# Two transformer blocks on one core: a raised priority for the attention strips' vector and scalar work, and half of each stacked key tile copied by DMA

## The chip, the cores and the metric

The kernel runs on one core of a Trainium2 chip. Its engines work side by side, each through its own instructions in order: TensorE (PE, with its weight loads as PEld), VectorE (DVE), ScalarE (ACT), GpSimd (POOL) and SyncE (SP, which here only issues DMAs). The metric is the device time of one execution in microseconds (us); lower is better.

## What is computed

A first block and then a second one run over a sequence of 512 positions with a model width of 1024; the sums are in float32. The first block has softmax attention with 8 heads of 64 columns beside a gated unit, the second has 8 heads of banded "chunk attention" (ca) and 8 heads of latent attention (mla). Each block ends in a convolutional feed-forward network. Cut to what matters here:

```python
def forgetting_attention(q, k, v, log_f):            # block 1, 8 heads of 64
    logits = einsum('bqhd,bkhd->bhqk', qi, k) * scale + ci[..., None] - c_k
    logits = where(causal, logits, -inf)
    p = softmax(logits); return einsum('bhqk,bkhd->bqhd', p, v)

def chunk_attention(q, k, v, rel_bias):              # block 2, 8 heads of 64; q, k are normed
    s = einsum('bqhd,bkhd->bhqk', qch, kb) * scale + bias[None]
    p = softmax(where(valid, s, NEG_INF)); return einsum(..., p, vb)

def second_block(...):
    q = rmsnorm_2(x w_q ...); k = ...; o_mla = mla_attention(q, k, v)
    cq, ck = rmsnorm_2(ca[0]), rmsnorm_2(ca[1]); o_ca = chunk_attention(cq, ck, cv, rel_bias)
    x = x + g_a * concat(o_mla, o_ca) @ w_out;  ...conv feed-forward...
```

## The kernel before

**Matrix products.** Every large product is made of three products of fp32r parts: a float32 matrix is split into a high part (`whi`, `xnh`) and the rest (`wlo`, `xnl`), and high·high, high·low and low·high are summed in PSUM (L369 is the one line that issues matmuls). ACT casts the high part of a weight piece (L347), DVE or POOL subtracts for the low part (L348). SP loads the raw pieces into three `wraw` buffers (L338).

**Attention strips.** A strip is one head and 128 query rows, `qi` 0 to 3, with 128 to 512 keys. In the order of time a strip is: the score matmuls (`strip_scores`, `s<-kh,qs` and `s<-kl,qs`), a DVE pass that adds the bias and takes the row minimum (L590, `s<-s,bs`, in an order's rows ISA, in the profile CUSTOM_DVE_ANT_0), the exponential on ACT (L594, `p<-s,st`), transposes on PE (L603, `s<-ident,p`), a copy to SBUF on ACT or DVE, whichever the scheduler gives it to (L605, `pt<-s`), and the product with the values (`o<-vc,pt`). `attention` walks over all strips. In turn t it issues the scores of strip t, then half of its `fill`, the transposes of strip t-1, the other half of `fill`, and the values of strip t-2. `fill` is a list of other matrix products (in block 2: `cq1`, `ck1`, `mla0`, `cv1`, `mla1`, parts of the output projection), and `rate(t)` says how many ns of it a turn takes. `bg` is a list of background work on DVE, ACT and POOL, above all norms; `bg` runs 60 places behind in priority. A norm ends in a power on POOL (`rsqrt`, L523), between a scale on DVE and the products on DVE that use it (`ca<-ca,ssc` L1423, `mqk<-mqk,nw` L1514).

**Stacked heads.** In block 1 and for the ca heads, `stack` builds for each head `qs` (high part of q in one half of the partitions, low part in the other), `kh` (the high part of k in both halves) and `kl` (the low part of k in both halves). Each half is 64 partitions by 512 floats, 128 KB. Head h is prepared `ahead` strips before its first strip: 2 in block 1, 4 in block 2.

**What sets the order.** PE runs in the order of the program. On the other engines a scheduler sets the order when the program is built: it takes the ready instruction of the best priority by its own estimates of time. On the chip each engine then runs that order strictly, so an instruction that waits holds up all behind it.

## Time and profile before

| | |
|---|---|
| median of 3 runs | 1244.67 us (1243.74 to 1245.11) |
| the profiled execution's own time | 1242.75 us |
| its span, first to last instruction | 1240.9 us |
| mean granted TensorE clock | 0.989 |
| TensorE matmul busy | 97% of the span |
| VectorE, ScalarE, GpSimd busy | 64%, 43%, 16% |

All times in rows are microseconds from the start of the span. Idle time of an engine counts only where PE, the engine that is nearly always busy, waits for it. A row's "granted clock" (PEclk) of 1.00 is 2.4 GHz and of 0.50 is 1.2 GHz.

### The profile page before, as it was taken

Reading aid. Unit: us, or ns where it says so; the run is one execution under the profiler, and the core shown is the slowest. Engines: PE = TensorE matmul, PEld = TensorE weight load, DVE = VectorE, ACT = ScalarE, POOL = GpSimd, SP = SyncE. Lnnn points to the kernel's source line nnn. Section 1 sums busy time; section 2 is a strip of 40 time slices with the busy share of each in tenths; the row PEclk is TensorE's granted clock in tenths of the full one; section 3 lists DMA queues with packets and bytes.
Section 4 is the critical chain, followed back from the end, with each engine's and each line's share of the span. In section 5 each row is a group of like instructions: output and inputs, shape, how many; then the busy total and the mean of one; then the engine's idle time right before and its main releaser. Section 6 shows DMA issues by size and latency. Waiting matters only on the chain.

```text
span 1240.9 us, 17330 instructions
## 1 busy us (share of the span) xinstructions
PE 1206.9 (97%) x6730; PEld 1049.5 (85%) x6730; DVE 792.5 (64%) x1415; ACT 539.2 (43%) x963; POOL 194.2 (16%) x208
## 2 busy tenths in 40 slices
PE   9999999999999999999998998899999999999998
PEld 6887878988888888888998897789988888888887
DVE  6555877688888886433666779766676566553221
ACT  6444544444444443223435555664554444442110
POOL 1457400300000000000344452501200000000000
PEclk9999999999999999999999999999999999999999
DMA  7321212156666656433122111110132222233330
GB/s 242 99 86 48 73 68 69 52 190 200 189 202 195 193 185 193 129 94 114 56 103 64 56 69 61 51 35 18 69 119 87 101 102 92 96 94 103 117 110 17
DMA packets 40033, 131.57 MB, mean 106 GB/s; under 512 B 4608, under 2 KB 5504, under 8 KB 39952
## 3 DMA queue, kind: packets, MB, share of 16 engines
q1 hardware_dynamic: 31536, 102.64, 25.2%
q10 hardware_dynamic: 8208, 27.27, 7.1%
q8 instruction: 52, 0.85, 0.3%
q0 software_dynamic: 208, 0.57, 0.2%
q14 instruction: 29, 0.24, 0.1%
HBM read 128.37 MB, written 2.10 MB: 105 GB/s over the span
## 4 chain that ended last, share of the span: by engine, by line
PE 85%; DVE 7%; POOL 4%; ACT 2%; issue 2%; DMA 1%; SPq 0%; POOLq 0%; ACTq 0%; DVEq 0%
PE mm L369 74%; PE s L369 4%; PE o L369 3%; PE s L603 2%; DVE wlo L348 1%; DVE nt L550 1%; DMA x<-in_xT_dram 1%; DVE ca L1423 1%; DVE s L590 0%; POOL ss L523 0%; POOL nw L523 0%; PE s L695 0%; DVE kl L669 0%; DMA cs<-in_c_dram 0%; PE mm L1635 0%
## 5 line engine op out<-in xcount | busy, mean ns | idle before, releaser
L348 DVE TENSOR_TENSOR wlo<-wraw,whi 128x1024 fp32r<-128x1024 f32 (+4 forms) x182 | 210.4, 1158 | 182.0 <-ACT whi L347 181.2
L347 ACT CAST whi<-wraw 128x1024 fp32r<-128x1024 f32 (+4 forms) x194 | 192.2, 994 | 281.3 <-PE mm L369 261.8
L369 PE MATMUL mm<-xnh,whi 128*128 128x512 f32 (+1 forms) x832 | 312.4, 375 | 1.1 <-DVE nt L550 0.6
L369 PE MATMUL mm<-xnl,whi 128*128 128x512 f32 (+1 forms) x832 | 311.0, 374 | 0.0
L369 PE MATMUL mm<-xnh,wlo 128*128 128x512 f32 (+1 forms) x832 | 310.7, 373 | 0.0
L369 PEld LDWEIGHTS mm<-xnh,whi 128*128 128x128 f32 x832 | 157.0, 189 | 28.7 <-PE mm L369 0.8
L369 PEld LDWEIGHTS mm<-xnh,wlo 128*128 128x128 f32 x832 | 157.1, 189 | 27.7
L369 PEld LDWEIGHTS mm<-xnl,whi 128*128 128x128 f32 x832 | 157.2, 189 | 27.1
L369 PE MATMUL mm<-gh,whi 128*128 128x512 f32 (+1 forms) x384 | 141.6, 369 | 1.1 <-DVE x L937 0.6
L369 PE MATMUL mm<-gl,whi 128*128 128x512 f32 (+1 forms) x384 | 141.3, 368 | 0.0
L369 PE MATMUL mm<-gh,wlo 128*128 128x512 f32 (+1 forms) x384 | 141.3, 368 | 0.0
L729 DVE SCALAR_TENSOR_TENSOR cv<-mm,cols,cv 128x510 f32<-128x510 f32 (+1 forms) x176 | 130.4, 746 | 2.6 <-ACT cv L727 0.6
L369 PE MATMUL mm<-whi,xnh 128*128 128x256 f32 (+3 forms) x304 | 97.7, 321 | 0.2 <-ACT xnh L812 0.2
L369 PE MATMUL mm<-wlo,xnh 128*128 128x256 f32 (+3 forms) x304 | 94.3, 310 | 0.2 <-DVE wlo L348 0.2
L369 PE MATMUL mm<-whi,xnl 128*128 128x256 f32 (+3 forms) x304 | 94.2, 310 | 0.1
L369 PEld LDWEIGHTS mm<-gh,whi 128*128 128x128 f32 x384 | 72.4, 188 | 13.6 <-DVE x L937 0.8
L369 PEld LDWEIGHTS mm<-gl,whi 128*128 128x128 f32 x384 | 72.4, 188 | 12.1
L369 PEld LDWEIGHTS mm<-gh,wlo 128*128 128x128 f32 x384 | 72.4, 188 | 12.0
L594 ACT ACTIVATE p<-s,st 128x128 f32<-128x128 f32 (+1 forms) x96 | 50.7, 528 | 69.7 <-DVE st L590 66.7
L998 DVE CUSTOM_DVE_ANT_0 wada<-wada,cs,cols 128x1024 f32<-128x1024 f32 x48 | 61.5, 1282 | 26.9 <-DMA wada<-in_w_ada_dram 26.7
L369 PE MATMUL mm<-mix,whi 128*128 128x256 f32 (+1 forms) x288 | 74.4, 346 | 2.7 <-ACT vm L1563 1.2
L727 ACT ACTIVATE cv<-mm,cols 128x512 f32<-128x512 f32 x88 | 67.6, 772 | 0.2 <-PE mm L369 0.2
(293 smaller groups left out, 1839.1 us busy)
## 6 DMA issues: line engine op xcount, KB each, us to landing
wraw<-in_w_up_dram SPq DMA_DIRECT2D x88, 512.0 KB, 3.4
wada<-in_w_ada_dram ACTq DMA_DIRECT2D x48, 512.0 KB, 3.6
wraw<-in_w_down_dram SPq DMA_DIRECT2D x32, 512.0 KB, 3.5
wraw<-in_w_out_dram SPq DMA_DIRECT2D x16, 512.0 KB, 3.4
wraw<-in_w_down_dram SPq DMA_DIRECT2D x16, 384.0 KB, 3.1
wraw<-in_w_qk_dram SPq DMA_DIRECT2D x8, 512.0 KB, 3.7
wraw<-in_w_v_dram SPq DMA_DIRECT2D x8, 256.0 KB, 4.9
x<-in_xT_dram SPq DMA_DIRECT2D x8, 256.0 KB, 6.4
```

What stands on the lines that cost most here:

```text
L347: nc.scalar.copy(hi[:, :n], raw[:, :n])
L348: (nc.gpsimd if pool else nc.vector).tensor_tensor(out=lo[:, :n], in0=raw[:, :n], in1=hi[:, :n].bitcast(F32), op=ALU.subtract)
L369: self.nc.tensor.matmul(out, lhsT, rhs, start=start, stop=stop, **kw)
L550: self.applied = nc.vector.scalar_tensor_tensor(out=t, in0=x[k][:, cs], scalar=gain(k), in1=r, op0=ALU.mult, op1=ALU.mult).ins
L594: nc.scalar.activation(out=p[:, :nk], in_=s[:, :nk], func=AF.Exp, bias=st[:, len(parts) - 1:len(parts)], scale=-1.0, accum_out=hd["sums"](qi))
L603: self.nc.tensor.transpose(s[:, c], p[:, c], self.ident)
L727: nc.scalar.activation(out=t, in_=ps, func=AF.Identity, scale=w[2], bias=self.col(cb, n))
L729: nc.vector.scalar_tensor_tensor(out=t[:, d:], in0=ps[:, :512 - d], scalar=w[2 - d], in1=t[:, d:], op0=ALU.mult, op1=ALU.add)
L998: nc.vector.tensor_tensor_reduce(out=w, in0=w, in1=self.cs, scale=1.0, scalar=self.col("b_ada_2", n), op0=ALU.mult, op1=ALU.add, accum_out ...
L1423: nc.vector.tensor_tensor(out=v3, in0=v3, op=ALU.mult, in1=ss[:, j, z, t].unsqueeze(2).to_broadcast([P, 4, 64]))
```

## The change

Four things change. (1) The DVE pass, the exponential, the copy `pt` and the two instructions that end a pair of heads (`reciprocal` and `att`) are recorded with a priority 150 places ahead. (2) In `stack`, the second half of `kh` and of `kl` is no longer computed by ACT and DVE but copied from the first half by a DMA on SP's queue. (3) In block 2, three rounds of 1200 ns of `fill` and 800 ns of `bg` are issued ahead of the attention, and (4) the fill between the first head's preparation and its first strip is 1500 ns instead of 3000 ns.

```diff
+FIRST = 150
 BEHIND = 60
...
-        for j, (cs, b) in enumerate(parts):
-            nc.vector.tensor_tensor_reduce(
...
-        p = self.pp.tile([P, 512], F32, tag="p", name="p")
-        nc.scalar.activation(out=p[:, :nk], in_=s[:, :nk], func=AF.Exp, bias=st[:, len(parts) - 1:len(parts)],
-                             scale=-1.0, accum_out=hd["sums"](qi))
+        with self.tc.high_priority(offset=FIRST):
+            for j, (cs, b) in enumerate(parts):
+                nc.vector.tensor_tensor_reduce(
...
+            p = self.pp.tile([P, 512], F32, tag="p", name="p")
+            nc.scalar.activation(out=p[:, :nk], in_=s[:, :nk], func=AF.Exp,
...
-        self.nc.any.tensor_copy(out=pt[:, :nk], in_=s[:, :nk])
+        with self.tc.high_priority(offset=FIRST):
+            self.nc.any.tensor_copy(out=pt[:, :nk], in_=s[:, :nk])
...
-        for o in (a, b):
-            nc.scalar.copy(kh[o], k[a])
-            nc.vector.tensor_tensor(out=kl[o], in0=k[a], in1=kh[a].bitcast(F32), op=ALU.subtract)
+        nc.scalar.copy(kh[a], k[a])
+        nc.vector.tensor_tensor(out=kl[a], in0=k[a], in1=kh[a].bitcast(F32), op=ALU.subtract)
+        for t in (kh, kl):
+            nc.sync.dma_start(out=t[b].bitcast(F32), in_=t[a].bitcast(F32))
...
-        nc.vector.reciprocal(sums[:, c8], sums[:, c8])
         att = self.att.tile([P, 512], F32, tag="att", name="att")
...
+        with self.tc.high_priority(offset=FIRST):
+            nc.vector.reciprocal(sums[:, c8], sums[:, c8])
+            nc.vector.tensor_tensor(out=att[:, c512].rearrange("p (g d) -> p g d", d=64),
...
+        for _ in range(3):
+            fill.run(1200)
+            bg.run(800)
         self.attention(
             heads, fill,
-            lambda t: 3000 if t < 0 else 2000 if t < 16 else 1600 if t < 34 else 500,
+            lambda t: 1500 if t < 0 else 2000 if t < 16 else 1600 if t < 34 else 500,
```

Three places in the orders of the engines show what moves: the norm of `ck1` on DVE and POOL, the preparation of a later pair of heads on DVE, and SP's queue. On PE the same instructions are issued; in block 2 there are 30 matmuls of 256 columns between the transposes of the first pair of heads (`mm<-ident,ca`) and the first score before, and 12 in the change, where 36 others have moved ahead of these transposes.

DVE in block 2, at the norm of `ck1`, before (`s<-s,bs` is a strip's bias pass, 128 to 512 keys wide; `ssc` is the norm's statistic):

```order
L590 ISA s,st<-s,bs 128x128
L590 ISA st 128x1
L348 TENSOR_TENSOR wlo<-wraw,whi 128x256
L1606 TENSOR_SCALAR bs<-bs 128x512
L1435 COPY ca<-mm 128x256 x2
L590 ISA s,st<-s,bs 128x256
...
L1412 TENSOR_REDUCE ssc<-sqc 128x4 x2
L1418 TENSOR_SCALAR ssc<-ssc 128x16
L1423 TENSOR_TENSOR ca<-ca,ssc 128x256 x3
L687 TENSOR_TENSOR att<-o,sums 128x512
L590 ISA s,st<-s,bs 128x384
```

The same place in the change:

```order
L592 ISA s,st<-s,bs 128x128
L592 ISA st 128x1
L1424 TENSOR_SCALAR ssc<-ssc 128x16
L1492 COPY mqk<-mm 128x384
L1429 TENSOR_TENSOR ca<-ca,ssc 128x256
L1612 TENSOR_SCALAR bs<-bs 128x512
L1429 TENSOR_TENSOR ca<-ca,ssc 128x256 x3
L592 ISA s,st<-s,bs 128x256
...
L1492 COPY mqk<-mm 128x384 x2
...
L693 TENSOR_TENSOR att<-o,sums 128x512
L592 ISA s,st<-s,bs 128x384
```

The norm stands one strip earlier, and the strip of 256 keys now stands behind its products instead of ahead of them.

POOL at the norm of `ck1`, before (`sqc` are its squares, `ssc<-ssc,nhalf` is its power, `wlo` the low part of a weight piece):

```order
L1411 TENSOR_TENSOR sqc<-ca 128x256 x2
L1607 MEMSET bs 64x64
L1411 TENSOR_TENSOR sqc<-ca 128x256 x2
L348 TENSOR_TENSOR wlo<-wraw,whi 128x1024
L523 TENSOR_TENSOR ssc<-ssc,nhalf 128x16
L348 TENSOR_TENSOR wlo<-wraw,whi 128x1024
```

The same place in the change:

```order
L1417 TENSOR_TENSOR sqc<-ca 128x256 x4
L524 TENSOR_TENSOR ssc<-ssc,nhalf 128x16
L349 TENSOR_TENSOR wlo<-wraw,whi 128x1024
L1613 MEMSET bs 64x64
L349 TENSOR_TENSOR wlo<-wraw,whi 128x1024
```

The power stands ahead of the weight split instead of behind it.

DVE a little later in block 2, where the third pair of ca heads (`qf`, `qs`, `kl`) is prepared, before:

```order
L1599 COPY qf<-mm 128x512
L348 TENSOR_TENSOR wlo<-wraw,whi 128x1024
L1606 TENSOR_SCALAR bs<-bs 128x512
L666 TENSOR_TENSOR qs<-qf,qs 64x512
L669 TENSOR_TENSOR kl<-kf,kh 64x512 x2
L590 ISA s,st<-s,bs 128x128
L590 ISA st 128x1
L590 ISA s,st<-s,bs 128x256
```

The same place in the change (`x` are products of the final norm of block 1):

```order
L1605 COPY qf<-mm 128x512
L592 ISA s,st<-s,bs 128x128
L592 ISA st 128x1
L349 TENSOR_TENSOR wlo<-wraw,whi 128x1024
L609 COPY pt<-s 128x512
L1612 TENSOR_SCALAR bs<-bs 128x512
L670 TENSOR_TENSOR qs<-qf,qs 64x512
L672 TENSOR_TENSOR kl<-kf,kh 64x512
L918 SCALAR_TENSOR_TENSOR x_83<-x_83,cols,mm 128x256
L918 SCALAR_TENSOR_TENSOR x_84<-x_84,cols,mm 128x256
L918 SCALAR_TENSOR_TENSOR x_85<-x_85,cols,mm 128x256
L592 ISA s,st<-s,bs 128x256
```

The strip of 128 keys has moved ahead of the weight split and of the head's preparation; the strip of 256 keys stands behind them and behind three products.

SP at the last two ca heads in the change, where before eight loads of `w_out` follow each other without a DMA between them (`kh<-kh` and `kl<-kl` are the new copies):

```order
L339 DMA wraw<-in_w_out_dram 128x1024 x4
L674 DMA kh<-kh 64x512
L674 DMA kl<-kl 64x512
L674 DMA kh<-kh 64x512
L339 DMA wraw<-in_w_out_dram 128x1024
L674 DMA kl<-kl 64x512
L339 DMA wraw<-in_w_out_dram 128x1024
```

The last head's `kl` copy stands behind a weight load that itself waits for a free `wraw` buffer.

## Rows read from the trace of the kernel before

**Rows 1.** The page: busy time, share of the span, instructions of an engine.

```profile
PE 1206.9 (97%) x6730; PEld 1049.5 (85%) x6730; DVE 792.5 (64%) x1415; ACT 539.2 (43%) x963; POOL 194.2 (16%) x208
```

**Rows 2.** Stretch, us, busy of PE, PEld, DVE, ACT, POOL; PEclk, DMA share, GB/s.

```profile
62.00:212.00 150.00, 142.10 (x804) 121.06 (x804) 101.67 (x252) 72.96 (x159) 55.52 (x53) 0.97 0.21 67
...
656.00:670.00 14.00, 10.60 (x76) 9.99 (x75) 11.30 (x14) 7.41 (x13) 5.19 (x3) 0.88 0.06 20
670.00:730.00 60.00, 54.90 (x423) 53.64 (x422) 43.19 (x100) 30.62 (x75) 29.94 (x34) 0.95 0.20 65
...
730.00:786.00 56.00, 48.55 (x329) 43.69 (x329) 49.02 (x112) 33.08 (x80) 20.81 (x22) 0.97 0.22 76
```

**Rows 3.** Waits of PE, 656 to 786: total us, times, longest.

```profile
PE s L603 <- ACT p L594: 8.6, 5, 2.9
PE mm L1596 <- DVE ca L1423: 3.4, 2, 2.2
```

**Rows 4.** Timeline of PE around the first score of block 2: start, length.

```profile
661.73 1.66 PE L1596 MATMUL mm<-ident,ca 128*128 128x128 f32 x6 [2.17 <-DVE ca L1423]
...
665.64 0.28 PE L369 MATMUL mm<-whi,xnh 128*128 128x256 f32 x1
...
667.57 0.28 PE L369 MATMUL mm<-whi,xnl 128*128 128x256 f32 x1
667.69 0.28 PE L369 MATMUL s<-kh,qs 128*128 128x256 f32 x1
```

**Rows 5.** Timeline of PE: the longest gaps after that, in brackets.

```profile
704.36 0.66 PE L695 MATMUL s<-ident,att 128*128 128x128 f32 x4 [1.53 <-DVE att L687]
...
705.97 0.50 PE L369 MATMUL s<-kh,qs 128*128 128x512 f32 x1 [0.78 <-DVE pt L605]
...
725.83 0.55 PE L603 MATMUL s<-ident,p 128*128 128x128 f32 x3 [2.46 <-ACT p L594]
...
749.28 0.33 PE L603 MATMUL s<-ident,p 128*128 128x128 f32 x1 [2.89 <-ACT p L594]
```

**Rows 6.** Timeline of DVE at the start of block 2's attention.

```profile
656.21 5.80 DVE L1423 TENSOR_TENSOR ca<-ca,ssc 128x256 f32<-128x256 f32 x4 [3.02 <-POOL ssc L523]
...
665.37 1.38 DVE L669 TENSOR_TENSOR kl<-kf,kh 64x512 fp32r<-64x512 f32 x2
```

**Rows 7.** Timelines of POOL and DVE at the norm of `ck1`.

```profile
697.16 2.40 POOL L348 TENSOR_TENSOR wlo<-wraw,whi 128x1024 fp32r<-128x1024 f32 x1
699.67 2.90 POOL L523 TENSOR_TENSOR ssc<-ssc,nhalf 128x16 f32<-128x16 f32 x1
...
697.69 1.90 DVE L1418 TENSOR_SCALAR ssc<-ssc 128x16 f32<-128x16 f32 x1
702.61 1.09 DVE L1423 TENSOR_TENSOR ca<-ca,ssc 128x256 f32<-128x256 f32 x3 [3.01 <-POOL ssc L523]
```

**Rows 8.** Timeline of DVE at the first norm of the mla queries.

```profile
723.52 0.96 DVE L1514 TENSOR_TENSOR mqk<-mqk,nw 128x768 f32<-128x768 f32 x1 [3.03 <-POOL nw L523]
724.40 0.56 DVE L590 CUSTOM_DVE_ANT_0 s<-s,bs 128x384 f32<-128x384 f32 x1
```

**Rows 9.** Timeline of DVE where the third pair of ca heads is prepared.

```profile
745.91 2.46 DVE L669 TENSOR_TENSOR kl<-kf,kh 64x512 fp32r<-64x512 f32 x2
748.29 0.28 DVE L590 CUSTOM_DVE_ANT_0 s<-s,bs 128x128 f32<-128x128 f32 x1
```

**Rows 10.** Groups by shape: count, busy us, mean ns of one, idle before.

```profile
L669 DVE TENSOR_TENSOR kl<-kf,kh 64x512 fp32r<-64x512 f32 x32 | 24.7, 771 | 0.6
...
L605 DVE COPY pt<-s 128x384 f32<-128x384 f32 x7 | 3.9, 554 | 0.3 <-PE s L603 0.3
```

**Rows 11.** DMA issues: count, KB each, median us from issue to landing.

```profile
wraw<-in_w_v_dram SPq DMA_DIRECT2D x8, 256.0 KB, 4.9
...
wraw<-in_w_kv_dram SPq DMA_DIRECT2D x2, 128.0 KB, 2.1
out_dram<-x SPq DMA_DIRECT2D x2, 128.0 KB, 1.7
```

More of the change, by code (lines that the diff above doesn't have):

```diff
@@ L588, in strip_scores @@
         parts = hd["bias"](qi)
-        for j, (cs, b) in enumerate(parts):
-            nc.vector.tensor_tensor_reduce(
-                out=s[:, cs], in0=s[:, cs], in1=b, scale=1.0, scalar=3e38 if j == 0 else st[:, j - 1:j],
-                op0=ALU.add, op1=ALU.min, accum_out=st[:, j:j + 1])
-        p = self.pp.tile([P, 512], F32, tag="p", name="p")
-        nc.scalar.activation(out=p[:, :nk], in_=s[:, :nk], func=AF.Exp, bias=st[:, len(parts) - 1:len(parts)],
-                             scale=-1.0, accum_out=hd["sums"](qi))
+        with self.tc.high_priority(offset=FIRST):
+            for j, (cs, b) in enumerate(parts):
+                nc.vector.tensor_tensor_reduce(
+                    out=s[:, cs], in0=s[:, cs], in1=b, scale=1.0, scalar=3e38 if j == 0 else st[:, j - 1:j],
+                    op0=ALU.add, op1=ALU.min, accum_out=st[:, j:j + 1])
+            p = self.pp.tile([P, 512], F32, tag="p", name="p")
+            nc.scalar.activation(out=p[:, :nk], in_=s[:, :nk], func=AF.Exp,
+                                 bias=st[:, len(parts) - 1:len(parts)], scale=-1.0,
+                                 accum_out=hd["sums"](qi))
         return s, p
@@ L684, in pair_end @@
         c8, c512 = slice(2 * qs[0], 2 * qs[-1] + 2), slice(qs[0] * P, (qs[-1] + 1) * P)
-        nc.vector.reciprocal(sums[:, c8], sums[:, c8])
         att = self.att.tile([P, 512], F32, tag="att", name="att")
-        nc.vector.tensor_tensor(out=att[:, c512].rearrange("p (g d) -> p g d", d=64),
-                                in0=o[:, c512].rearrange("p (g d) -> p g d", d=64),
-                                in1=sums[:, c8].unsqueeze(2).to_broadcast([P, 2 * len(qs), 64]),
-                                op=ALU.mult)
+        with self.tc.high_priority(offset=FIRST):
+            nc.vector.reciprocal(sums[:, c8], sums[:, c8])
+            nc.vector.tensor_tensor(out=att[:, c512].rearrange("p (g d) -> p g d", d=64),
+                                    in0=o[:, c512].rearrange("p (g d) -> p g d", d=64),
+                                    in1=sums[:, c8].unsqueeze(2).to_broadcast([P, 2 * len(qs), 64]),
+                                    op=ALU.mult)
         def turn():
```

## The prediction

> **What bounds the kernel now.** I read the page first: PE is busy for 1206.9 of 1240.9 us [rows 1], so only its idle time, 34 us, and the time at the lower clock can be won. Then the busy time by stretch, to see where that idle time lies. In the attention of block 2, 656 to 786, PE is idle for 14 - 10.60 = 3.4, 60 - 54.90 = 5.1 and 56 - 48.55 = 7.45 us, 15.95 us in all [rows 2]. The granted clock costs more: (1 - 0.88) x 14 = 1.7, (1 - 0.95) x 60 = 3.0 and (1 - 0.97) x 56 = 1.7 us, 6.4 us in all, which is time at 1.2 GHz behind the longer gaps. In the attention of block 1, 62 to 212, PE is idle for 7.9 us and the clock costs 0.03 x 150 = 4.5 us. The waits of PE then say for whom it waits in block 2: the transposes of strips wait for the exponential for 8.6 us in five gaps, and the first transposes of the ca heads wait 3.4 us for a norm [rows 3]. Last come the timelines of PE and DVE around each of these gaps, to see which instruction was late.
>
> **The change part by part, in block 2.** The sum is made against the profiled execution, 1242.75 us; the median of the three runs is 1.9 us above it. I price a gap that goes with the clock behind it: two gaps in 670 to 730 go with 3.0 us of lost clock, so 1.5 us each, and one in 730 to 786 goes with 1.7 us [rows 2, 5].
>
> *(a) The start.* PE waits 1.23 and 2.17 us, 3.4 in all, for the four products `ca`, which end at 656.21 + 5.80 = 662.0 [rows 3, 6]. In the change 36 matmuls come first. Their pace at full clock is (667.57 - 665.64) / 17 = 0.114 us [rows 4], so they take 4.1 us and PE comes to the transposes when `ca` is done. That wait goes. But only 12 matmuls are left between the transposes and the first score, 1.4 us, and the score now waits for a DMA. Before, the transposes ended at 663.4 (661.73 + 1.66), and the first of the two `kl` halves at 665.37 + 0.69 = 666.06, 2.7 us later [rows 4, 6]. No row shows a copy inside SBUF. The nearest rows are loads and stores of the same 128 KB, 2.1 and 1.7 us from issue to landing, and as a far bound a load of 256 KB in a burst of others, 4.9 us [rows 11]. I take 2.1, because nothing else is in flight at that place. With the transposes over at 662.9 the score can start at 662.9 + 2.7 + 2.1 = 667.7, and I allow 0.3 us for the issue on SP: 668.0. It stood at 667.69 [rows 4]. So it is 0.3 us later, with 18 more matmuls (2.05 us) done: a gain of 1.75 us, and 2.1 or -1.1 us by the ends 1.7 and 4.9. The idle time is about the same 3.5 us, and so is its clock; it has moved from the norm to the DMA.
>
> The Trainium skill (SBUF — State Buffer, "Door 1: The DMA port swizzle" and "The DMA setup-cost knee") gives about 2 us of fixed cost, and for 64 partitions only half of the ports, 218 GB/s. By this the copy would take an estimated 2 + 131072 / 218000 = 2.6 us, and the gain at (a) would be 1.25 us instead of 1.75. No row here shows a copy between partitions.
>
> *(b) The norm of `ck1`.* DVE's scale took 1.90 us beside POOL's weight split, then its products waited 3.01 us for POOL's power of 2.90 us, and `att` and the strip of 384 keys stood behind them [rows 7]. PE lost 1.53 and 0.78 us there, and the clock 1.5 [rows 5, 2]. In the change POOL does the power ahead of the weight split, so the 1.9 us should go, and the norm stands one strip earlier. Now the strip of 256 keys is behind the products. From the strip before it that is 1.0 to the scale, 0.2 for it, 2.9 of power and 2.1 of products, copy and bias: its pass starts 6.3 us after the earlier strip's score and its exponential is done 1 us later, at 7.3. Strips follow each other by about 3.4 us, and a strip's transposes come about 1.3 strips after its score, so they are due at 3.4 + 4.4 = 7.8: just in time. `att` is ready 2 us later and is due one strip later. Gain 2.3 + 1.5 = 3.8 us, and nothing if it is late.
>
> *(c) The first mla norm.* The strip of 384 keys stood behind a product that waited 3.03 us for POOL, and PE lost 2.46 us [rows 8, 5]. In the change the statistics are done a strip earlier, a `kl` of the next head fills part of the wait, and the strip of 256 keys is behind the product; by the same count as at (b) it is late by some 0.2 us. Gain 2.3 + 1.5 = 3.8 us.
>
> *(d) The third pair of heads.* The strip of 128 keys stood behind a weight split, a bias, `qs` and two `kl` products of together 2.46 us, and PE lost 2.89 us [rows 9, 5]. In the change it stands ahead of them all. Gain 2.9 + 1.7 = 4.6 us.
>
> *(e) What is given back.* From 730 to 786 DVE is busy for 49.0 of 56 us [rows 2]. The 16 `kl` halves are worth 16 x 0.77 = 12.3 us over the whole kernel, of which the four heads of this stretch have 3.1; but 12 copies `pt` move from ACT to DVE, 6.6 us at 0.55 [rows 10], about half of them here. So DVE still needs nearly 49 us there, and strips that come up to 9 us earlier find it in arrears. The strip of 256 keys at (d) now waits for seven instructions instead of none. I count one gap of the size of the 1.53 us one with its clock, 3.0 us, and the 2.05 us of matmuls that (a) took ahead and that cover nothing here: 5.1 us.
>
> *Block 1.* The passes of the strips stand in the same order on DVE as before, on PE nothing moves, and the heads are prepared two strips of (212 - 62) / 32 = 4.7 us ahead, 9.4 us against a copy of 2.1. I count zero; if one of its gaps goes, -3, if one copy comes late, +2.
>
> *SP's queue.* 32 issues are added to a queue on which loads wait for `wraw` buffers. A copy behind such a load is as late as that load. The worst place is the last head's `kl`, behind a load of `w_out`. The buffer for that load is freed by a weight split that stands five rows ahead of this `kl` on DVE, so the load is issued before the copy is ready. I count zero, covered by the two to four strips of lead; without that cover a head costs 2.1 us.
>
> **Sum.** (b), (c) and (d) give 12.2 us. They hang on counts that come within 0.5 us of being late, so I take 80% of them, 9.8. With 1.75 for (a) and -5.1 for (e) that is a gain of 6.4 us: 1236.3 against the profiled execution, 1238 against the median.
>
> **The rivals.** *Nothing moves.* The gaps close where they were and open at the next strip, because DVE is what the strips wait for and its work in 656 to 786 is hardly smaller. For it speaks that 49.0 of 56 us is nearly full and that DVE runs in order; against it that from 670 to 730 it is busy for only 43.2 of 60 us [rows 2]. Then (b) to (e) cancel and (a) is lost again later: 1243.5 to 1245.
>
> *Slower: strips behind the power on POOL.* The priority can't take a strip past an instruction that already waits on DVE. In the change three strips stand behind a product that waits 2.9 us for POOL (at the norms of `ck1` and of both mla queries), where before two cost PE time [rows 7, 8]. Each costs 2.5 us and 1.5 of clock if it is exposed. If all three are, and a fourth at the norm of `cq1`, where a `pt` copy now stands behind the products, that is 16 us instead of the 7.6 of (b) and (c). With (d) and (a) kept and (e) paid it is 16 - 7.6 - 4.6 + 5.1 - 1.75 = 7.2 us slower; with three of the four, 3.2 slower. It decides where a strip's transposes are due less than about 4.4 us after its score. The middle of the two: 1249.5.
>
> *More.* (e) doesn't come, because (b) to (d) leave DVE in step: 1.75 + 12.2 = 14 us, 1231. Against it speaks DVE's share from 730 on.
>
> **Chances.** My forecast has 48%, with a range of its own from 1234 to 1242; nothing moves 20%; slower 18%; more 14%. A measurement of this kernel can tell 0.2%, 2.5 us, from no change. Of my forecast 46 of the 48 are faster and 2 within it; of "nothing moves" 3 are faster, 14 within and 3 slower; of the slower case 1 is within. So faster 0.63, within 0.17, slower 0.20. The range of 1231 to 1247 leaves out half of the slower case and a little of "more".
>
> **What would show each step.** (a) no wait for `ca`, and a gap of about 3.5 us before the first score of block 2, ended by a DMA, with a landing near 2.1 us. (b) POOL's power straight behind the squares and no gap at `att`. (c) the gap at the first mla norm under 1 us. (d) no gap over 1 us at the first strip of the third pair. (e) one new gap between strips 18 and 28, and DVE over 90% busy there. The prediction is wrong if copies land later than 3 us, if new waits of matmuls for `kh` or `kl` show up elsewhere, or if the clock in 656 to 786 is below 0.95.

## The result: 0.6% slower

The change takes 1251.7 us (median of four executions, 1250.43 to 1252.75) where the kernel before takes 1244.9: a ratio of 1.0059, interval 1.0044 to 1.0074. Faster had the larger chance in the prediction, at 1238; the measured time lies outside its range. The profiled execution has a span of 1250.8 us against 1240.9, so 9.9 us have to be found in the trace.

### The profile page after: what moved, and what is told of

It reads as the page before. It is cut to its first block, busy times and chain, and to the rows that moved or that the text cites. A ratio compares the mean times of both kernels' runs of the same rounds, so it can differ in the third digit from the quotient of the medians.

```text
span 1250.8 us, 17404 instructions
## 1 busy us (share of the span) xinstructions
PE 1210.1 (97%) x6730; PEld 1052.5 (84%) x6730; DVE 786.8 (63%) x1413; ACT 523.3 (42%) x933; POOL 192.5 (15%) x208
## 4 chain that ended last, share of the span: by engine, by line
PE 85%; DVE 6%; ACT 3%; POOL 3%; issue 2%; DMA 2%; SPq 0%; ACTq 0%; DVEq 0%; POOLq 0%
PE mm L370 75%; PE s L370 4%; PE o L370 3%; PE s L606 2%; DVE wlo L349 1%; ACT whi L348 1%; DVE s L592 1%; PE mm L1641 1%; ACT p L596 1%; DMA x<-in_xT_dram 1%; DMA cs<-in_c_dram 0%; POOL ss L524 0%; POOL sqg L1099 0%; PE s L701 0%; POOL wlo L349 0%
```

## The profile after

The page's first line: busy time, share and instructions of each engine.

```profile
PE 1210.1 (97%) x6730; PEld 1052.5 (84%) x6730; DVE 786.8 (63%) x1413; ACT 523.3 (42%) x933; POOL 192.5 (15%) x208
```

DVE and ACT have less to do, by 5.7 and 15.9 us, as the diff promises [rows 1]. PE has the same instructions, is busy 3.2 us longer (the same matmuls at a lower clock) and idle 6.7 us longer. To see where, the span is cut at the same matmuls in both kernels: the first score of block 1, its last `att` transposes, the start of block 2, the first score of block 2, the last wait of block 2's output projection. The columns are those of [rows 2]; the last line is a stretch by itself. First the kernel before:

```profile
0.00:71.20 71.20, 67.73 (x326) 54.44 (x327) 44.13 (x77) 37.62 (x60) 23.53 (x32) 0.98 0.49 156
71.20:219.05 147.85, 141.43 (x833) 121.69 (x831) 99.24 (x253) 72.39 (x160) 53.18 (x53) 0.98 0.21 68
219.05:603.38 384.33, 382.79 (x1924) 326.85 (x1925) 267.10 (x396) 152.70 (x225) 14.01 (x16) 1.00 0.51 160
603.38:667.69 64.31, 60.65 (x470) 59.78 (x471) 43.09 (x101) 27.25 (x57) 31.20 (x27) 0.95 0.20 66
667.69:871.57 203.88, 189.65 (x1413) 178.06 (x1411) 153.36 (x363) 115.82 (x288) 63.75 (x71) 0.97 0.16 53
871.57:1240.90 369.33, 364.69 (x1770) 308.66 (x1770) 185.55 (x230) 133.41 (x177) 8.51 (x11) 1.00 0.27 92
756.00:800.00 44.00, 40.64 (x275) 35.17 (x274) 38.05 (x92) 24.58 (x64) 14.88 (x16) 1.00 0.16 55
```

and then the change:

```profile
0.00:69.80 69.80, 65.87 (x325) 53.07 (x326) 42.70 (x75) 36.40 (x58) 23.23 (x32) 1.00 0.53 167
69.80:218.09 148.29, 141.41 (x833) 121.57 (x832) 98.37 (x253) 65.97 (x148) 52.94 (x53) 0.98 0.26 79
218.09:606.00 387.91, 384.28 (x1925) 328.33 (x1925) 267.15 (x396) 152.63 (x225) 13.99 (x16) 1.00 0.51 158
606.00:669.87 63.87, 60.88 (x489) 60.26 (x489) 42.72 (x101) 27.19 (x56) 32.95 (x29) 0.97 0.21 69
669.87:878.09 208.22, 191.44 (x1393) 179.14 (x1393) 150.34 (x363) 107.89 (x273) 60.91 (x70) 0.96 0.20 61
878.09:1250.80 372.71, 366.19 (x1770) 310.15 (x1770) 185.51 (x230) 133.23 (x177) 8.46 (x11) 1.00 0.28 91
756.00:800.00 44.00, 35.32 (x207) 30.06 (x206) 35.49 (x84) 20.09 (x51) 13.64 (x15) 0.88 0.17 58
```

The lengths differ by -1.4, +0.4, **+3.6**, -0.4, **+4.3** and **+3.4** us. Three stretches carry the loss. One is the strips of block 2, of which the prediction spoke. The other two, 7.0 us together, lie where an attention stage hands over to a feed-forward network, of which it said nothing. A handover is here the place where the next stage's first products take over PSUM banks of the stage ahead. The waits there, in PE's timeline of the kernel before:

```profile
233.12 0.39 PE L369 MATMUL mm<-xnh,whi 128*128 128x256 f32 x1 [0.46 <-DVE x L847]
...
873.89 0.36 PE L369 MATMUL mm<-xnh,whi 128*128 128x256 f32 x1 [0.64 <-DVE nt L550]
```

and of the change:

```profile
234.25 0.39 PE L370 MATMUL mm<-xnh,whi 128*128 128x256 f32 x1 [2.54 <-DVE x L853]
...
882.30 0.36 PE L370 MATMUL mm<-xnh,whi 128*128 128x256 f32 x1 [2.51 <-ACT sq L494]
```

Both waits are about 2 us longer than before, and the rest of 3.6 and 3.4 us is the clock behind them: from 234.25 to 240 and from 882.30 to 888 the granted clock is 0.70 in the change, 1.7 us each, and in the 6 us behind the same two matmuls before it is 1.00. DVE does the same as before at the first of these places, in the same order and pace. Of its last three sums `x` (called x5, x6 and x7 below), the first in the kernel before:

```profile
232.66 0.41 DVE L847 TENSOR_TENSOR x<-mm,x 128x256 f32<-128x256 f32 x1
```

and the first and the third in the change:

```profile
231.69 0.41 DVE L853 TENSOR_TENSOR x<-mm,x 128x256 f32<-128x256 f32 x1
...
233.79 0.41 DVE L853 TENSOR_TENSOR x<-mm,x 128x256 f32<-128x256 f32 x1
```

The matmul that waited for the first of the three before (232.66 + 0.41 = 233.07, PE at 233.12) waits for the third of them now (233.79 + 0.41 = 234.20, PE at 234.25). Why, the built programs show: in which of the eight PSUM banks each product lies.

```
                    banks of the last products that x5, x6, x7 read | first two products of the network
before, block 1     5, 7, 4                                         | 0, 5: the second waits for x5
change, block 1     7, 4, 5                                         | 0, 5: the second waits for x7
before, block 2     2, 3, 1                                         | 0, 5: the first waits for a row of the norm
change, block 2     1, 2, 0                                         | 0, 5: the first waits for x7
```

At the second handover the profile's row names a square on ACT, but in the built program the wait of that matmul that comes last is the one for x7 on DVE, which ends at 881.67 + 0.48 = 882.15 us (change):

```profile
881.67 0.48 DVE L930 SCALAR_TENSOR_TENSOR x<-mm,mod,x 128x256 f32<-128x256 f32 x1
```

The pool gives its four `mm` banks out in another order, from the 53rd of 423 tiles on, though PE's own rows in block 1 are unchanged. In the change the bank that is read last is, at both handovers, one of the two that the next stage writes first.

Back in block 2, the longest waits of PE from 656 to 786 (total, times, longest):

```profile
PE s L606 <- ACT p L596: 9.5, 5, 3.4
PE s L370 <- DMA kh<-kh: 2.7, 1, 2.7
PE mm L370 <- DVE x L918: 2.5, 1, 2.5
```

The 3.4 us for `ca` are gone and the first score waits for its copy instead, but the strips wait 9.5 us for the exponential where it was 8.6 [rows 3]. The gaps in PE's timeline:

```profile
669.87 0.36 PE L370 MATMUL s<-kh,qs 128*128 128x256 f32 x1 [2.73 <-DMA kh<-kh]
...
707.50 0.44 PE L606 MATMUL s<-ident,p 128*128 128x128 f32 x2 [1.62 <-ACT p L596]
...
725.75 0.44 PE L606 MATMUL s<-ident,p 128*128 128x128 f32 x2 [3.43 <-ACT p L596]
...
759.57 0.70 PE L370 MATMUL mm<-mix,whi 128*128 128x512 f32 x2 [2.45 <-DVE x L918]
...
770.14 0.33 PE L606 MATMUL s<-ident,p 128*128 128x128 f32 x1 [2.21 <-ACT p L596]
...
781.25 0.66 PE L606 MATMUL s<-ident,p 128*128 128x128 f32 x4 [1.85 <-ACT p L596]
```

The gap of 3.43 is longer than the 2.46 at the same norm before [rows 5], and from 756 to 800 PE is idle for 8.7 us at a clock of 0.88, where it was 3.4 us at 1.00. Two of the causes show on DVE and ACT. (A third is that of 781.25: at the second mla norm too a strip's pass stands behind a product that waits for POOL's power, 1.60 us.) At the first mla norm the strip of 256 keys stands behind the product that waits for POOL's power:

```profile
723.74 0.96 DVE L1520 TENSOR_TENSOR mqk<-mqk,nw 128x768 f32<-128x768 f32 x1 [2.81 <-POOL nw L524]
724.62 0.42 DVE L592 CUSTOM_DVE_ANT_0 s<-s,bs 128x256 f32<-128x256 f32 x1
...
764.64 0.30 DVE L592 CUSTOM_DVE_ANT_0 s<-s,bs 128x128 f32<-128x128 f32 x1 [1.53 <-PE s L370]
...
769.04 0.55 DVE L1507 TENSOR_REDUCE nw<-sqm 128x4 f32<-128x384 f32 x1
```

And at 765 a strip's pass is done, but its exponential starts only at 769.63, when a reduction for the next norm is over (ACT):

```profile
769.63 0.37 ACT L596 ACTIVATE p<-s,st 128x128 f32<-128x128 f32 x1 [3.32 <-DVE nw L1507]
```

The exponential's output `p` and the norm's squares `sqm` share three buffers. The reduction that frees one has no raised priority and stands behind a weight split, a head's preparation and another raised strip.

## The experiments

Two questions, each with two answers. *Where is the time lost?* **Theory 1:** the handovers of PSUM banks, by rows 7.0 us. **Theory 2:** the strips; a wait at a handover only spends what the next stage would wait for anyway. *Why don't the strips gain?* **Theory P:** the raised exponential waits for a buffer that low-priority work holds. **Rival B:** DVE is in arrears, and what one strip gains the next loses; as part of this, the copies `pt`, of which twelve more lie on DVE. In the table every ratio is against the kernel before on the same chip. "Banks" says whether an early product of a stage gets a bank that the stage ahead reads late; the order of the PSUM pools alone was altered for it. "Good" has two orders for the pools of block 2 (c3), so runs that differ in it are no pair of one edit: `s=3, mm=4, o=1` in e9, e10, e11 and e16, and `s=3, o=1, mm=4` in e5, e7, e12, e15 and e17; e6, e8 and e18 leave c3 alone.

| run | kernel | banks | median, us | ratio | interval |
|---|---|---|---|---|---|
| | change | two bad | 1251.70 | 1.0059 | 1.0044 to 1.0074 |
| e13 | change again | two bad | 1254.17 | 1.0078 | 1.0052 to 1.0104 |
| e14 | change | one bad | 1252.84 | 1.0065 | 1.0044 to 1.0085 |
| e1 | change | one bad, at the start of block 2 | 1252.38 | 1.0065 | 1.0048 to 1.0082 |
| e5 | change | good | 1247.94 | 1.0035 | 1.0016 to 1.0053 |
| e6 | before | good | 1244.58 | 0.9992 | 0.9977 to 1.0008 |
| e2 | before | one bad, at the start of block 2 | 1248.63 | 1.0038 | 1.0025 to 1.0051 |
| e3 | before | two bad | 1249.68 | 1.0039 | 1.0025 to 1.0053 |
| e4 | priority alone | one bad, at the start of block 2 | 1255.16 | 1.0077 | 1.0056 to 1.0098 |
| e7 | priority alone | good | 1248.01 | 1.0027 | 1.0008 to 1.0045 |
| e8 | copies by DMA alone | good | 1241.09 | 0.9966 | 0.9949 to 0.9983 |
| e18 | the same again | good | 1241.79 | 0.9974 | 0.9958 to 0.9990 |
| e11 | fill ahead alone | good | 1241.48 | 0.9973 | 0.9958 to 0.9989 |
| e10 | change without priority | good | 1243.87 | 1.0005 | 0.9990 to 1.0021 |
| e16 | e10, first pair of heads not copied | good | 1240.81 | 0.9965 | 0.9949 to 0.9981 |
| e17 | e5, `pt` not raised | good | 1243.69 | 0.9988 | 0.9969 to 1.0006 |
| e9 | change, squares in own buffers | good | 1245.67 | 1.0001 | 0.9985 to 1.0018 |
| e15 | e7, squares in own buffers | good, but 1.28 us at the last | 1246.05 | 1.0016 | 0.9996 to 1.0035 |
| e12 | copies alone, squares in own buffers | good | 1243.12 | 0.9991 | 0.9972 to 1.0009 |

**The banks, first attempt (e1 to e4).** The pools of both attention stages in another order; in e3 `mm` first in block 1 and last in block 2.

```diff
-            self.open_psum(c1, s=3, o=1, mm=4)
+            self.open_psum(c1, o=1, mm=4, s=3)
...
-            self.open_psum(c3, mm=4, s=3, o=1)
+            self.open_psum(c3, o=1, mm=4, s=3)
```

> The changed kernel with the PSUM pools of the two attention stages opened in another order, so that the first two products of each feed-forward network take banks that the last products of the attention stage did not use. The orders of all five engines are the same as in the change. Theory 1 (the change lost its time at the two handovers of banks): the waits of 2.54 and 2.51 us shrink to about 0.4, and the half-clock period behind each goes: 2.1 + 1.9 + 2 x 1.7 = 7.4 us less than 1251.7, so 1244.3, with a further 1 us at most because the waits get shorter than in the kernel before: 1243.3 to 1244.5. Theory 2 (the time is lost in the strips and the handover only spends slack that the next stage would lose anyway): 1250 to 1252.

> The kernel before with the same order of PSUM pools, orders of all engines unchanged. Theory 1: its waits at the two handovers were only 0.46 and 0.64 us, with no half-clock period behind them, so 0 to 1.1 us are to be had: 1243.6 to 1244.9. Theory 2: no change, 1244.9.

> The kernel before with PSUM pools opened so that the first product of the first feed-forward network, and the second product of the second one, take the bank of the last product of the attention stage. Theory 1: the first waits until the last x is added, 235.2 instead of 232.15 us, 3.0 us, with 1.7 of clock, in place of 0.46; the second until 875.7 instead of 874.2, 1.5 us, with or without 1.7 of clock: 5.7 to 7.5 us slower, 1250.6 to 1252.4. Theory 2: 1244 to 1246.

> The raised priority alone (keys computed as before, no fill ahead of the attention of block 2), with free banks. If the priority itself costs time, because strips stand behind the power on POOL and DVE's backlog comes later: over 1246.5. If its gains and its losses cancel: 1243 to 1245, as the kernel before with free banks. If the order of DVE is what helps and the other parts of the change spoil it: under 1241.

e1 missed by 8 us, and its trace says why: the two waits are gone, and a new one stands at the third handover, where block 2 starts (PE, e1):

```profile
605.25 0.55 PE L370 MATMUL s<-xnh,whi 128*128 128x256 f32 x1 [6.47 <-DVE nt L551]
```

There the kernel before and the change wait 0.57 us. The new order of block 2's pools puts its second product on a bank whose row the norm of all eight `x` still reads. So e1, e2 and e4 have one bad handover instead of two or none, and e2 shows its price on the kernel before: 1.0038 against 0.9992 with good banks (e6; each against the kernel before on its own chip), 0.46% or 5.7 us, about the 5.9 us by which the wait grew in e2 (6.46 against 0.57). In e3 (PE) the waits came out as forecast, or longer:

```profile
235.13 0.36 PE L369 MATMUL mm<-xnh,whi 128*128 128x256 f32 x1 [3.00 <-DVE x L847]
...
881.45 0.39 PE L369 MATMUL mm<-xnh,whi 128*128 128x256 f32 x1 [2.08 <-DVE x L924]
```

The kernel before, with the orders of its engines unchanged but for a few small instructions ahead of block 2, got 0.39% slower, 4.9 us, a little under the forecast. Theory 1's mechanism is shown by time on the kernel before, and on the changed kernel by the waits of e1's trace. e4 could not be read by itself.

**Good banks at all three (e5 to e8).** c1 as above in all four; in e5 and e7 c3 opened as `s=3, o=1, mm=4`, in e6 and e8 left alone.

> The changed kernel with PSUM pools ordered so that none of the three handovers of banks (attention of block 1 to its feed-forward network, from there to block 2, attention of block 2 to its network) gives an early product the bank of a late one; apart from one pair of small instructions on DVE and on POOL ahead of block 2 all engines keep their orders. Theory 1 (of the change's loss, 7.4 us lie at the handovers: 2.1 + 1.9 of wait and 2 x 1.7 of clock): 1243.5 to 1245.5, that is no measurable difference to the kernel before. Theory 2 (the loss is in the strips): 1250 to 1252.

> The kernel before with the PSUM pools of the first attention stage in another order, all engines' orders unchanged, and nothing altered at the two later handovers. Only the wait of 0.46 us at its first handover can go: 1244 to 1245, by both theories. Much above that would say that the order of the pools costs time in some other way.

> The raised priority alone, with good banks at all three handovers. In the earlier run of it the handover into block 2 took 6.47 us with 6.8 us at half clock, where the kernel before waits 0.8 with 3.4: 5.6 + 1.7 = 7.3 us. By theory 1 these go: 1243 to 1248, and what is then above or below 1244.6 is what the order of the strips is worth by itself. By theory 2: 1250 to 1255.

> The copies by DMA alone (no raised priority, no fill ahead, 3000 ns of fill at the start), with good banks at all three handovers. A copy lands 2.2 us after its issue. If that only hits the first score of each block and the 12 us less work on DVE don't count: the first score of block 2 comes 2 us later, 1245 to 1247. If DVE is what the strips of 730 to 786 wait for, the work taken from it shows: 1240 to 1243.

e5 lies between the theories. Its trace has no wait over 0.2 us in the first products of either network, and the stretch around the first shows it; the change and then e5:

```profile
212.00:236.00 24.00, 20.22 (x164) 19.75 (x164) 15.95 (x37) 12.61 (x27) 7.59 (x11) 0.98 0.08 23
```

```profile
212.00:236.00 24.00, 22.81 (x193) 22.54 (x192) 15.58 (x39) 13.36 (x29) 7.95 (x11) 1.00 0.14 47
```

But only 0.24% of the change's loss went by the first measurement and 0.43% by its repetition (e13), 3.0 to 5.4 us, and e5's interval meets that of either, so for the changed kernel itself the time only points the way that the traces show. What is left is 0.35%. The parts alone then gave the surprise: priority costs 0.27%, copies give 0.34%, fill ahead gives 0.27% (e11, below). Good banks against one bad handover are worth 0.50% to the priority alone (e7, e4), with intervals apart.

**One handover alone (e13, e14).** e14 has only the first line of the diff above.

> The changed kernel itself, so that it stands beside the next one on the same chip: 1.0044 to 1.0074 of the kernel before, as measured.

> The changed kernel with the PSUM pools of the first attention stage in another order, so that only the first handover gets good banks; the orders of all engines and all banks of block 2 are those of the change, the bad handover at the end of block 2 included. Theory 1: 2.5 us of wait and 1.2 to 1.7 of clock less than the changed kernel beside it, 3.7 to 4.2 us, about 0.3% of the time. Theory 2: the same time as the changed kernel.

The wait at the first handover is gone in e14's trace, the second stands at 2.52 us, and the time is 0.13% less than the change beside it (e13, itself a little above its forecast). That points the way of theory 1 at less than half its size, and the intervals overlap: one handover alone is not resolved by time.

**Buffers (e9, e15, e12).**

```diff
-                sq = self.pp.tile([P, 512], F32, tag="p", name="sqm")[:, :4 * d]
+                sq = self.pp.tile([P, 384], F32, tag="sqm", name="sqm", bufs=2)[:, :4 * d]
```

> The changed kernel with good banks, and with two buffers of their own for the squares of the mla norms (sqm), which in the change take one of the three buffers that the strips' exponentials (p) use. Theory P (the priority is upset by a shared buffer: the raised exponential of the strip of 128 keys waits until a reduction of the squares, which is not raised, has run on DVE): the gap of 2.2 us at about 769 goes, and with it one or two half-clock periods of 3.4 us, 1.7 us each: 3.9 to 5.6 us under the 1247.9 of the same kernel with shared buffers, 1242.3 to 1244. Rival B (DVE is simply in arrears there, and the same time is lost at the next strip): 1246.5 to 1249.

> The raised priority alone with good banks (1.0027 of the kernel before when it was run), and the squares in buffers of their own. Theory P (a raised exponential waits for a buffer held by work that is not raised): the gap of 3.0 us at about 776 goes with the clock behind it, 3.0 + 1.7 to 3.4 us: 0.998 to 0.9995. Rival B (arrears of DVE, lost at the next strip instead): 1.0015 to 1.004.

> The copies by DMA alone, good banks, and the squares of the mla norms in buffers of their own: a candidate to beat both kernels. If shared buffers only hurt where the strips have a raised priority: no better than the copies alone, 0.996 to 0.998 of the kernel before. If they also hold up strips that are not raised: 0.993 to 0.996.

In e9 the wait at 770 is gone and the change comes to the time of before, between the two forecasts, though a strip at another norm (706.26) now waits 3.34 us where e5 has 1.62. That the buffers made it faster is not shown: its interval meets e5's, c3 is in another order, and in the profiled executions the strips of block 2, from the first score to the last wait of the output projection, take 210.07 us in e9 and 210.06 in e5. In e15 the wait of 3.0 us at 776 is gone too, but ten us later stands a longer one than any strip had before (PE, e15):

```profile
786.37 0.48 PE L606 MATMUL s<-ident,p 128*128 128x128 f32 x1 [4.98 <-ACT p L596]
```

so there rival B was right, and e15's time lies in its range, though with 1.28 us at the last handover that e7 has not. For the copies alone own buffers gained nothing (0.9991, above both forecasts). The shared buffer holds one exponential up, as theory P says; that freeing it makes the kernel faster in general is not shown, since the squares' new freedom reorders all of DVE's work behind them.

**The parts of the change together (e10, e11, e16, e17).** e10 is the change without the raised priority, e11 the fill ahead alone. e16 is e10 with the following, where `copied` is false for the first pair of heads of each block alone,

```diff
+        if copied:
             nc.scalar.copy(kh[a], k[a])
...
+        else:
+            for o in (a, b):
+                nc.scalar.copy(kh[o], k[a])
+                nc.vector.tensor_tensor(out=kl[o], in0=k[a], in1=kh[a].bitcast(F32), op=ALU.subtract)
```

and e17 is e5 with

```diff
-        with self.tc.high_priority(offset=FIRST):
-            self.nc.any.tensor_copy(out=pt[:, :nk], in_=s[:, :nk])
+        self.nc.any.tensor_copy(out=pt[:, :nk], in_=s[:, :nk])
```

> The change without the raised priority (copies by DMA, fill ahead of block 2, 1500 ns at the start), with good banks. If the priority is what costs and the other two parts add up: the copies alone gave 4.2 us, the fill ahead should give the 1.75 us of the prediction's step (a): 1238.5 to 1241. If the fill ahead bares the first copy, a gap of 2.7 us with clock behind it where the kernel before has 3.4 us, and gives nothing: 1240.5 to 1243. Over 1244 would say that the fill ahead costs time.

> The fill ahead of block 2 and the 1500 ns alone, keys computed as before, no raised priority, good banks. The 3.4 us of waiting for ca go; the first score then waits for the keys' halves on DVE, which come 0.5 to 2 us after the matmuls ahead of it are done. 1.5 to 3 us to the good at the start and 2.05 us of fill missing later: 1242 to 1245. If it costs time in the strips: over 1246.

> The change without the raised priority, good banks, and the keys of the first pair of heads of each block computed as before; only those of later pairs are copied by DMA. If the two helpful parts (copies 0.9966 alone, fill ahead 0.9973 alone) came to 1.0005 together because the fill ahead bares the first copy: the wait of 2.75 + 0.41 us at the first score of block 2 falls to 1.1 + 0.6 and one half-clock period goes, 1.5 + 1.7 = 3.2 us or 0.26%: 0.996 to 0.999. If they spoil each other in the strips behind it: 1.000 to 1.002.

> The change with good banks and with the copies pt left at their old priority; the DVE pass, the exponential, reciprocal and att stay raised. If the priority costs because 12 copies go from ACT to DVE, which is 6.6 us more work there: 1.000 to 1.002. If it costs by the order in which raised strips and norms stand on DVE: 1.002 to 1.005, as with raised copies (1.0035).

> The copies by DMA alone with good banks once more, as the fastest version so far: 0.995 to 0.998 of the kernel before, if it holds on this chip too; 0.999 or more if the first result was luck of the clock.

e10 gives nothing, though its two parts give 0.27 to 0.34% alone. The first score of block 2 in e10 and then in e16 (PE):

```profile
670.30 0.55 PE L370 MATMUL s<-kh,qs 128*128 128x256 f32 x1 [2.75 <-DMA kh<-kh]
```

```profile
667.12 0.38 PE L370 MATMUL s<-kh,qs 128*128 128x256 f32 x1 [1.11 <-ACT kh L678]
668.09 0.56 PE L370 MATMUL s<-kl,qs 128*128 128x256 f32 x1 [0.59 <-DVE kl L679]
```

With 12 matmuls of cover the copy's landing is bare; computing the first pair's halves makes e16 0.40% faster than e10, more than the forecast of 0.26%, and intervals that don't touch. e16 and e8 are the fastest kernels of the study, some 4 us under the kernel before; e18 repeats e8 within its forecast.

e17 is the clearest result on the priority. Leaving `pt` alone takes 0.47% off e5, 5.8 us, again with intervals apart, and more than either forecast allowed. All copies `pt` on DVE, before, change and e17 (count, then shortest, median and longest in ns, first and last start):

```profile
L605 DVE COPY pt<-s x21: 281/547/692, 76.9 to 847.4; 128x384 f32<-128x384 f32 x7, 128x128 f32<-128x128 f32 x6, 128x256 f32<-128x256 f32 x4, 128x512 f32<-128x512 f32 x4
```

```profile
L609 DVE COPY pt<-s x33: 273/425/692, 75.6 to 853.9; 128x128 f32<-128x128 f32 x10, 128x384 f32<-128x384 f32 x9, 128x256 f32<-128x256 f32 x7, 128x512 f32<-128x512 f32 x7
```

```profile
L608 DVE COPY pt<-s x25: 273/543/692, 76.3 to 849.0; 128x512 f32<-128x512 f32 x7, 128x128 f32<-128x128 f32 x6, 128x256 f32<-128x256 f32 x6, 128x384 f32<-128x384 f32 x6
```

Eight copies (4 of 128 columns, 1 of 256, 3 of 384), some 3 us of DVE, are not 5.8 us of the kernel by themselves. The order moved too: in e17 the strip of 256 keys at the mla norm passes ahead of the product that waits for POOL (DVE, e17).

```profile
721.85 0.43 DVE L592 CUSTOM_DVE_ANT_0 s<-s,bs 128x256 f32<-128x256 f32 x1
...
724.63 1.83 DVE L1519 TENSOR_TENSOR mqk<-mqk,nw 128x768 f32<-128x768 f32 x2 [2.29 <-POOL nw L524]
```

PE waits 0.16 us for this strip where e5 has 3.93, but then 1.51 and 2.43 us for the next two, for which e5 doesn't wait: 4.1 us in all. There the gap was only cut in pieces. From the first score of block 2 to the last wait of its output projection, e5 and then e17:

```profile
667.19:877.25 210.06, 193.83 (x1393) 181.10 (x1393) 150.49 (x363) 107.70 (x273) 60.92 (x70) 0.94 0.21 61
```

```profile
669.68:873.22 203.54, 188.25 (x1393) 176.07 (x1393) 148.87 (x359) 108.08 (x277) 60.42 (x70) 0.98 0.20 63
```

PE's idle time differs by 0.9 us only; the same matmuls take 5.6 us less at the higher clock. So in these two executions what raising `pt` costs is nearly all clock. That shorter gaps keep the clock up (the longest wait for an exponential there is 2.4 us in e17 and 3.9 in e5) is likely, but no run tests it.

## Why the prediction was wrong, by its steps

**What had no term: the handovers of banks.** The working stops at the ends of the attention stages; for block 1 it says that on PE nothing moves and counts zero. PE's rows did not move there, their operands' banks did, and with them the waits. By rows it is 7.0 us of the profiled 9.9. By time it is 3.0 to 5.4 us of the change's loss, and 0.4 to 0.5% where one kernel was run with good and with bad banks (e6 with e2 and e3, e7 with e4). The chance of "slower" had no mechanism of this kind. Against the profiled execution the forecast is off by 9.9 + 6.4 = 16.3 us: 7.0 are these handovers, 10.3 lie in block 2 up to its output projection (+3.9 instead of -6.4, steps (a) to (e)), and the rest, 0.4 less 1.4, in block 1 and ahead of it. How the pool picks a bank I infer from the programs, not from a run.

**(a) The start: the path right, the gain too large.** The wait for `ca` is gone. The gap moved to the first score and is 2.73 + 0.59 = 3.3 us (3.5 forecast). From the start of block 2 to its first score the change takes 0.44 us less with 18 more matmuls done, 2.05 us by the prediction's pace: a gain of 2.5 where 1.75 stood. But 1.7 of it is clock that was only moved: the kernel before loses it ahead of its first score (661.73 to 667.69, granted clock 0.71, then 1.00), the change behind it (664 to 669.87 at 1.00, then 0.72 up to 676). That leaves 0.8 us. The prediction said that the clock moves with the gap, and still compared the two first scores. The landing of the copies, the first unknown, was bounded well by its median, though the slowest took 4.7 us, later than the 3 us named as a sign of being wrong; only the first copies made PE wait. The 16 of `kh` in the change (count, KB each, median us from issue to landing; the 16 of `kl` have the same):

```profile
kh<-kh SPq DMA_DIRECT2D x16, 128.0 KB, 2.2
```

The Trainium skill's estimate for such a copy (SBUF — State Buffer, "Door 1: The DMA port swizzle" and "The DMA setup-cost knee") was 2.6 us; measured are 2.2, so the estimate was 0.4 us too long. What (a) did not see is that the same 3.3 us were avoidable: computing the first pair is worth 0.40% where the priority is not raised (e16).

**(b) The norm of `ck1`: half right.** No gap at `att`, but the strip of 256 keys, "just in time" by my count, came 1.62 us late. When it was due I had right. But its pass started 8.2 us after the earlier strip's score (698.15 to 706.37) instead of 6.3. POOL's power came as forecast; the first of the four products behind it did not (change, POOL and then DVE):

```profile
699.54 2.90 POOL L524 TENSOR_TENSOR ssc<-ssc,nhalf 128x16 f32<-128x16 f32 x1 [0.82 <-DVE ssc L1424]
702.41 2.41 POOL L349 TENSOR_TENSOR wlo<-wraw,whi 128x1024 fp32r<-128x1024 f32 x1
```

```profile
702.48 2.63 DVE L1429 TENSOR_TENSOR ca<-ca,ssc 128x256 f32<-128x256 f32 x1 [2.55 <-POOL ssc L524]
...
705.36 1.08 DVE L1429 TENSOR_TENSOR ca<-ca,ssc 128x256 f32<-128x256 f32 x3
```

It starts with POOL's weight split (702.41 to 704.82), takes 2.63 us and ends 0.3 us after it; the three others take 1.08 us together. The weight split that I saw leave the scale now lies on the product. The Trainium skill (SBUF — State Buffer, "Who interferes with whom") says that a DVE instruction with two SBUF inputs contends with a GpSimd instruction that reads SBUF; the trace agrees, with 2.63 us against about 0.4. So of the 2.3 us of idle time 0.7 is gained; its clock is too: from 707.50 to 716 the granted clock is 1.00.

**(c) The first mla norm: wrong.** Forecast was a strip late by 0.2 us; measured is a gap of 3.43 us in place of 2.46. The count again held for the due time and not for the pass, which started at 724.62, 10.4 us after the earlier strip's score (714.25) instead of 6.3. The norm's scale came only at 720.17, since the fourth reduction stood behind a bias that waited 1.28 us for its load and behind a `qs`; the power took 3.28 us. Here the rival of strips behind the power on POOL was right, at its price of 2.5 us and more.

**(d) The third pair: right.** The gap of 2.89 us and the clock behind it are gone; PE goes through the strip of 128 keys without a wait (751.91 us), and from 749 to 754 the granted clock is 1.00.

**(e) What is given back: the term of block 2 that was too small.** I counted one gap of 1.53 us with its clock, 3.0, and 2.05 of fill. From 756 to 800 alone PE is idle 5.3 us longer than before, and the clock of 0.88 costs up to 0.12 x 44 = 5.3 us more: as much as 10.6 us instead of 3.0. The sign for arrears of DVE did not come: it is busy for 35.5 of these 44 us, 81% and not over 90%. PE waits behind work that was not raised: a buffer of squares (2.21 us at 770.14), a bank that eight of the products `x` read (2.45 us at 759.57), a power on POOL (1.85 us at 781.25). And the twelve moved copies `pt` were priced by their 6.6 us of DVE alone, where e17 has 5.8 us of the kernel's time for eight of them, most of it clock.

**The sum and the rivals.** "80% of (b) to (d), less (e)" gave -6.4 us; block 2 measured is -0.4 + 4.3 = +3.9. The rival "slower" is right in a part: of its four strips behind POOL's power three are exposed (1.62 us at the norm of `ck1`, 3.43 and 1.85 at the two mla norms), and for three it says 3.2 us slower, near these 3.9. That the whole change measured 6.8 us slower by the medians, near the 7.2 that it says for four, is luck, since it knows nothing of the handovers. With good banks and `pt` left alone the change is at 0.9988 (0.9969 to 1.0006), no measurable difference. At 1243.7 us this lies in the range of the rival "nothing moves", but it is another kernel, and that gaps only move on there is not shown for the whole of it.

**What stays open.** Whether the raised pass and exponential help at all: e17 against e10 is 0.17% in their favour, inside the intervals, and c3 differs. How much of the change's loss the handovers are lies between 3.0 us by time and 7.0 by rows. And why e5's strips lost more at the lower clock than the change's own, with the same orders, is not settled.

## What to carry to other kernels

A change of priorities on one engine also moves which buffers and banks the pools give to others; after such a change compare the first waits of every stage, not only of the one that was edited, and open PSUM pools so that the first tiles of a stage never lie on the last tiles of the one ahead. Leave copies that may run on either of two engines out of such a raise, and look which buffers the raised work shares with work that is not raised; whether to raise that work too, no run here tried. Parts that gain 0.3% each may share one cover: test them together, and compute what is needed first instead of copying it.

## What the runs showed of the hardware

The same wait does not always cost its clock. PE waits 2.04 us for `cum` at 64.2 in the kernel before and 2.02 us at 64.5 in the change; from 64 to 68 the mean granted clock is 0.59 in the one

```profile
64.00:68.00 4.00, 3.79 (x9) 2.89 (x10) 3.86 (x8) 2.27 (x4) 0.48 (x1) 0.59 0.30 108
```

and 1.00 in the other:

```profile
64.00:68.00 4.00, 3.53 (x15) 2.74 (x16) 3.24 (x6) 1.39 (x2) 1.61 (x3) 1.00 0.75 220
```

That is (1 - 0.59) x 4 = 1.6 us, more than the whole 1.4 us by which the change seems faster up to its first score: luck, not the edit. All twenty traces have this wait, 2.01 to 2.04 us; in the 4 us behind it the granted clock is 1.00 in eleven of them and 0.57 to 0.68 in nine, and kernels with equal orders stand on both sides (before and e3 at 0.57, e2 and e6 at 1.00; the change, e13 and e14 at 1.00, e1 at 0.57, e5 at 0.65). The Trainium skill (TensorE: Matmul & The Clock Gate, "Part 1: The HAM clock gate") says that the window in which activity is judged runs freely and does not start with the kernel, and the traces fit that, with equal gaps that cost the clock in nine of twenty; the window itself no trace shows. Executions of one kernel here lie up to 12 us apart (e17: 1236.4 to 1248.7), so a difference of 0.3% needs many of them, and a clock term worked out from one profile carries an uncertainty of the size of a gap.
